# A 128-column stationary operand used as four 32-column quarters, and a copy that goes from ScalarE to VectorE, in a hybrid encoder layer

## Chip, cores and metric

The kernel runs on one core of a Trainium2 chip. The metric is the device time of one execution in microseconds (us). A core has five engines that run their own instruction queues side by side: TensorE (PE, with its weight loads shown apart as PEld), VectorE (DVE), ScalarE (ACT), GpSimd (POOL), and SyncE (SP), which here does nothing but issue DMAs. TensorE writes its results to PSUM, from where DVE and ACT take them to SBUF.

## The reference, cut to what matters

One encoder layer is applied to a prompt of 256 rows and to a sample of 2048 rows of width 1024. After a norm and one wide projection, half of the width goes through neighbourhood attention, the other half through a Fourier mix; both are normed, gated, projected out, normed again and added to the input.

```python
def fourier_mix(u, w_f, b_f):
    b, s, _ = u.shape
    ug = u.astype(jnp.float32).reshape(b, s, F_GROUPS, F_GROUP_DIM)
    spec = jnp.fft.fft2(ug, axes=(1, 3), norm='ortho')
    mixed = spec.real.reshape(b, s, F_WIDTH).astype(u.dtype)
    return mixed @ w_f + b_f

def encoder_layer(x, ...):
    h = rms_norm(x, g_pre)
    q, k, v, z_a, u_f, z_f = jnp.split(h @ w_in, ...)
    y_a = neighbourhood_attention(q, k, v, rpb)
    y_f = fourier_mix(u_f, w_fourier, b_fourier)
    mixed = jnp.concatenate([rms_norm(y_a, g_na) * jax.nn.silu(z_a),
                             rms_norm(y_f, g_f) * jax.nn.silu(z_f)], axis=-1)
    return x + rms_norm(mixed @ w_out, g_post)
```

Everything is float32. [...]

## The kernel before, in words

The program is written in the order in which TensorE works; until the third stage below the tile framework chooses the order on the other engines, except where a stretch is marked as ordered by hand. The stages in time:

1. Projections (0 to 549 us of the profile): norm, the products with `w_in`, and the first Fourier step. Results are kept in DRAM tiles (`kD`, `qD`, `vD`, `zD`, `ZD`, `uD`). Weight splits, masks and the rest of the preparation run beside it.
2. Second Fourier step (549 to 577 us, lines 1009 to 1080). `ZD` holds the first step's result, and four quarters of it, `zgs[0]` to `zgs[3]`, are loaded as four tiles of 128 x 512 each. For each quarter `gq` (called gq0 to gq3 here) and each block `c` of the 512 columns, `stage2` makes one PSUM tile `pab` of 128 x 4 x 64: four calls of `dft`, each with 128 columns of a `zg` tile as the standing operand and 64 columns of the table `d2` as the moving one. Block c = 4 is another kind: it takes 32 columns, every eighth from 256 on, and makes the same product three times, into three quarters of the partitions (c4 below). gq0 has a small extra product `pny` of one column in every block, gq2 one named `pup` of 129 columns with two accumulated matmuls. Each `pab` is then taken out of PSUM by `split_ps`: a rounded copy to `abh` (on ACT, on DVE for the first three blocks of gq0) and then the remainder to `abl` on DVE; the PSUM tile is free after the second. The tiles come from three buffers in turn (pool tag "b" has two, "c" one), so that a block waits for the third one before it to be taken out. Between the quarters stand the products `ppq` (`pq(0)` after gq2, `pq(1)` and `pq32` after gq3), which need the matrix `wf`.
3. Third Fourier step (577 to about 610 us, `y_mm` and `y_out`): for each of four row blocks e, three column tiles; PSUM buffers `py1` (three) and `py2` (two); DVE combines them into a tile `Y` (two buffers), which SP stores to DRAM. So the third `Y` (e = 2) can only be written once the store of the first has landed.
4. Attention (610 to about 860 us, the loop over `k` at line 1574), 36 groups, with the output products of the Fourier half (`po`) between them. Here the order on all engines is the order of the code. At eight places `norm_sums` adds up squares by matmuls with a matrix of ones, four standing quarters of 32 columns into `ptb[0]`, and copies the sums to SBUF (`nsb`, line 1481); `norm_turn` uses them in the next turn of the loop. `ptb[0]` is also what the next turn's transposes (`transp`, line 1505) write first, so that these wait for the copy.
5. Output products of the attention half and the last norm (860 to 969 us).

All DMAs of these stages are issued by SP in program order over eight semaphores in turn: an issue waits until the DMA eight issues before it has landed. Names in the DMA rows: `wf` is the Fourier weight (line 1005), `kl` the keys of the first head pair (line 1091, two halves), which `split_k` (line 1095) then casts on ACT in four parts to `kh`; `wo` are eight tiles of output weights (line 1234), whose buffers were those of `d2` and `zg` and so come free as TensorE goes on.

Of the kernel before, what the change touches and what calls it, by code (L numbers as in the profile page):

```python
# [168 lines left out]
def build(tc, A, O):  # L169
    nc = tc.nc  # L170
# [46 lines left out]
    def mmt(n):  # L217
        x = mmc[0] % 5 > 2
        mmc[0] += 1
        return ps.tile([128, n], F32, tag="t" if x else "a", name="mm", bufs=2 if x else 3)  # L220
# [539 lines left out]
    for b in range(16):  # L760
# [13 lines left out]
        if 2 <= b < 8:  # L774
            x, y = divmod(b, 2)
# [7 lines left out]
        p = mmt(512)[:, :TP]  # L783
# [3 lines left out]
        o = st.tile([128, 256], F32, tag="f", name="f", bufs=3)  # L787
        if kind % 2:
            i, d = p, o
        else:  # L790
            i = p.rearrange("p (b r c) -> p b r c", b=2, c=32)
            d = o.rearrange("p (r b c) -> p b r c", b=2, c=32)
# [46 lines left out]
    for i in range(16):  # L839
# [15 lines left out]
        o = [st.tile([128, 1024], F32, tag="f", name="f", bufs=3) for x in range(2)]  # L855
# [32 lines left out]
        for j in range(7):  # L888
# [29 lines left out]
            if sg == 0:  # L918
                x, y = divmod(7 * (pr - 1) + j, 14)
# [17 lines left out]
            for f, d in ((u_load, 0), (u_split, 4), (u_stage1, 6)):  # L937
                x = 7 * pr + j - 7 - d
# [11 lines left out]
            p = mmt(512)  # L950
# [39 lines left out]
    ptb = [ps.tile([128, 512], F32, tag="t", name="ptb", bufs=2) for i in range(2)]  # L990
# [24 lines left out]
    def split_ps(dh, dl, src, vec=False):  # L1015
        nc.vector.tensor_copy(dh, src) if vec else nc.scalar.copy(dh, src)
        nc.vector.tensor_tensor(out=dl, in0=src, in1=dh.bitcast(F32), op=ALU.subtract)

    def dft(p, c, pairs):
        sts = [(p[32 * r:32 * r + 32], slice(256, 512, 8)) for r in range(3)] if c == 4 else \  # L1020
            [(p, slice(c * 128, c * 128 + 128))]
        for out, cols in sts:
            for x, (z, d) in enumerate(pairs):
                nc.tensor.matmul(out, z[:, cols], d, start=x == 0, stop=x == len(pairs) - 1)  # L1024


    def split_ab(gq, c, view, p):
# [7 lines left out]
    def stage2(gq, zg, c):  # L1035
        m = int(c in (2, 3))
        np_ = 96 if c == 4 else 128
        x = (gq * 5 + c) % 3 == 2
        p = ps.tile([np_, 4, 64], F32, tag="c" if x else "b", name="pab", bufs=1 if x else 2)
        for g in range(4):  # L1040
            dft(p[:, g, :], c, [(zg[g], d2[gq // 2][:, (gq % 2) * 4 + g, m * 64:m * 64 + 64])])
        split_ab(gq, c, lambda a: a[:, :1024].rearrange("p (k q g l) -> p q g k l", k=16, q=4, g=4)[:, gq],
                 p.rearrange("p g (k l) -> p g k l", l=4))
        if gq == 0:
            p = ps.tile([np_, 1], F32, tag="a", name="pny")
            dft(p, c, [(zg[0], dnyq[:, m:m + 1])])
            split_ab(gq, c, lambda a: a[:, 1024:1025], p)
        if gq == 2:
            p = ps.tile([np_, 129], F32, tag="a", name="pup")
            dft(p, c, [(up[:, t], f256[:, t, 129 * m:129 * m + 129]) for t in range(2)])  # L1050
            split_ab(gq, c, lambda a: a[:, 1025:1154], p)
# [192 lines left out]
    for t, (g, x) in enumerate(zip(G, (0, 640))):  # L1244
        g["w"] = []
        for c0, w in g["t"]:
            n = 2 * g["nr"] * w
# [228 lines left out]
    def norm_sums(sq, ts):  # L1476
        n = 32 * len(ts)
        for x, t in enumerate(ts):
            nc.tensor.matmul(ptb[0][32 * x:32 * x + 32, :128], ones32, sq[:, t * 128:t * 128 + 128], start=True, stop=True)
        o = sm.tile([128, 128], F32, name="nsb", bufs=1)[:n]  # L1480
        nc.scalar.copy(o, ptb[0][:n, :128])  # L1481
        nsb.append(o)

    def norm_turn(dst, ts):
# [89 lines left out]
    for k in range(2, len(G) + 1):  # L1574
# [21 lines left out]
        x = k // 2 + 1  # L1596
# [52 lines left out]
        if k + 1 in NT:  # L1649
            norm_sums(sqs if k < 31 else ysq, NT[k + 1])  # L1650
# [8 lines left out]
        if 32 <= k < 36:  # L1659
            x, d = k - 32, atiles[k - 32]  # L1660
# [122 lines left out]
```

## Time and profile before

| | us |
|---|---|
| median of three runs (lowest 971.94, highest 977.72) | 972.99 |
| the profiled execution | 970.48 |
| its span from the first to the last instruction | 968.7 |
| TensorE busy in the span | 958.9 |
| VectorE busy | 709.5 |
| ScalarE busy | 497.5 |
| GpSimd busy | 430.2 |

The mean clock granted to TensorE is 0.998 of full speed. The profiled execution is 1.8 us longer than its span, and 2.5 us below the median. Rows of a timeline give the start, the duration, the engine, the source line, the operation, what is written and read, the sizes, and how many instructions are merged into the row; a bracket at the end tells how long the engine had been idle and what ended it. "128\*32" before the size of a matmul means that 128 rows and 32 columns of the array are used.

### The profile page before, as it was taken

The page shows a single profiled execution, that of the slowest core. Times are in us where ns is not written, and L with a number is a line of the kernel's source. Part 1 is how long each engine was busy: PE and PEld are TensorE (multiplying, and loading weights), DVE is VectorE, ACT ScalarE, POOL GpSimd, SP SyncE. Part 2 cuts the span into 40 slices and gives each one's busy share as a digit, 9 for nine tenths or more (in the row PEclk, how much of TensorE's full clock was granted, in tenths as well). Part 3 has the DMA queues.
Part 4 walks back from the last instruction along what each step waited for, and adds up shares of the span by engine and source line. Part 5 has one row for each costly group of instructions (what it writes and reads, how often), then busy time and mean ns, then how long its engine had stood idle before and what let it go on. Part 6 is the DMA issues. An engine that isn't in the chain of part 4 may idle for free.

```text
span 968.7 us, 17031 instructions
## 1 busy us (share of the span) xinstructions
PE 958.9 (99%) x5769; PEld 801.0 (83%) x5769; DVE 709.5 (73%) x1306; ACT 497.5 (51%) x1078; POOL 430.2 (44%) x400
## 2 busy tenths in 40 slices
PE   9999999999999999999999999999999999999997
PEld 7889988888888888888888879887788888878886
DVE  6768987777986867787777446776665656649997
ACT  6836675433325533333344255677666776744443
POOL 3100003464752202756654033577677686624544
PEclk9999999999999999999999999999999999999999
DMA  9899696556849996599989898698887998979993
GB/s 327 312 373 357 234 366 240 194 189 252 318 163 377 352 410 239 211 371 320 322 303 339 301 328 300 210 281 273 258 240 234 286 327 270 296 244 331 330 346 129
DMA packets 146450, 279.89 MB, mean 289 GB/s; under 512 B 13162, under 2 KB 84284, under 8 KB 142972
## 3 DMA queue, kind: packets, MB, share of 16 engines
q1 hardware_dynamic: 145932, 278.41, 82.4%
q8 instruction: 46, 0.75, 0.3%
q10 hardware_dynamic: 432, 0.39, 0.1%
q14 instruction: 40, 0.33, 0.1%
HBM read 184.37 MB, written 101.72 MB: 295 GB/s over the span
## 4 chain that ended last, share of the span: by engine, by line
PE 96%; DVE 1%; ACT 1%; issue 1%; POOL 1%; DMA 0%; DVEq 0%; SPq 0%; POOLq 0%; ACTq 0%
PE po L1432 19%; PE mm L165 18%; PE mm L164 18%; PE mm L166 18%; PE pv L1521 5%; PE ptb L1505 5%; PE s L1181 4%; PE pab L1024 2%; PE py L164 1%; PE py L166 1%; PE py L165 1%; DMA gpre<-gpre 0%; PE ppq L1062 0%; PE pz L166 0%; PE pz L164 0%
## 5 line engine op out<-in xcount | busy, mean ns | idle before, releaser
L164 PE MATMUL mm<-xh,wa 128*128 128x512 f32 x448 | 174.4, 389 | 0.0
L165 PE MATMUL mm<-xl,wa 128*128 128x512 f32 x448 | 174.3, 389 | 0.0
L166 PE MATMUL mm<-xh,wa 128*128 128x512 f32 x448 | 174.3, 389 | 0.0
L536 POOL TENSOR_TENSOR ws<-wr 128x512 f32<-128x512 f32 x16 | 22.2, 1386 | 226.6 <-DMA wr<-wz 222.8
L1215 POOL TENSOR_SCALAR w<-w,m 128x480 f32<-128x480 f32 (+6 forms) x136 | 86.0, 644 | 46.3 <-DVE m L1212 35.9
L164 PEld LDWEIGHTS mm<-xh,wa 128*128 128x128 f32 x448 | 84.1, 188 | 17.6
L166 PEld LDWEIGHTS mm<-xh,wa 128*128 128x128 f32 x448 | 84.1, 188 | 17.5
L165 PEld LDWEIGHTS mm<-xl,wa 128*128 128x128 f32 x448 | 84.1, 188 | 17.4
L1432 PE MATMUL po<-wo,yh 128*128 128x512 f32 x272 | 90.4, 413 | 0.0
L551 DVE TENSOR_TENSOR wa<-wr,wa 128x512 fp32r<-128x512 f32 x60 | 68.5, 1149 | 27.1 <-ACT wa L550 26.8
L1208 ACT ACTIVATE w<-w,m 128x480 f32<-128x480 f32 (+6 forms) x136 | 79.3, 586 | 17.1 <-DVE m L1203 17.1
L1432 PE MATMUL po<-w,yh 128*128 128x512 f32 x280 | 86.7, 391 | 0.0
L1203 DVE CUSTOM_DVE_ANT_1 w<-s,tb 128x360 f32<-128x360 f32 (+5 forms) x124 | 62.4, 541 | 10.3 <-PE s L1181 9.8
L589 POOL TENSOR_TENSOR mt<-mt,rmask 128x880 f32<-128x880 f32 (+2 forms) x24 | 51.0, 2139 | 34.1 <-DVE mt L585 27.6
L165 PE MATMUL mm<-vl,xh 128*128 128x512 f32 x168 | 65.5, 390 | 0.2 <-DVE vl L482 0.2
L164 PE MATMUL mm<-vh,xh 128*128 128x512 f32 x168 | 65.4, 389 | 0.0
L166 PE MATMUL mm<-vh,xl 128*128 128x512 f32 x168 | 65.4, 389 | 0.0
L877 DVE TENSOR_TENSOR f<-u,mm 128x512 f32<-128x512 f32 x64 | 43.5, 680 | 28.0 <-PE mm L166 23.1
L1432 PEld LDWEIGHTS po<-w,yh 128*128 128x128 f32 x280 | 52.3, 188 | 10.9 <-issue 0.2
L1505 PE MATMUL ptb<-ident,w 128*120 128x128 f32 (+5 forms) x428 | 59.5, 276 | 1.0 <-ACT nsb L1481 0.9
L550 ACT CAST wa<-wr 128x512 fp32r<-128x512 f32 x60 | 36.4, 617 | 44.1 <-PE mm L166 23.2
L1521 PEld LDWEIGHTS pv<-pt,v 120*64 120x64 f32 (+6 forms) x896 | 48.2, 136 | 12.8 <-issue 9.6
(263 smaller groups left out, 2394.3 us busy)
## 6 DMA issues: line engine op xcount, KB each, us to landing
wr<-wz SPq DMA_DIRECT2D x48, 512.0 KB
vl<-sD SPq DMA_DIRECT2D x20, 512.0 KB
xm<-xm SPq DMA_DIRECT2D x9, 1024.0 KB
oD<-ofs SPq DMA_DIRECT2D x18, 512.0 KB
of<-oD SPq DMA_DIRECT2D x18, 512.0 KB
yr<-yD SPq DMA_DIRECT2D x34, 256.0 KB
zD<-f SPq DMA_DIRECT2D x16, 512.0 KB
woD<-wo SPq DMA_DIRECT2D x16, 512.0 KB
```

Source lines behind the costliest of these rows:

```text
L164: nc.tensor.matmul(out, lh, rh, start=first, stop=False)
L165: nc.tensor.matmul(out, lh, rl, start=False, stop=False)
L166: nc.tensor.matmul(out, ll, rh, start=False, stop=last)
L551: nc.vector.tensor_tensor(out=o[:, 1], in0=src, in1=o[:, 0].bitcast(F32), op=ALU.subtract)
L589: nc.gpsimd.tensor_tensor(out=o, in0=i, in1=rmask[:, m0:m0 + n].unsqueeze(2).to_broadcast([128, n, 80]), op=ALU.add)
L877: nc.vector.tensor_tensor(out=dst(f, b), in0=src(uu[u]), in1=src(p), op=op)
L1203: nc.vector.tensor_tensor_reduce(out=rows(g["w"][b][:, h, :n], w), in0=rows(g["s"][2 * b + h][:, :n], w), in1=tv, scale=1.0, scalar=3.0e38 ...
L1208: nc.scalar.activation(w, w, AF.Exp, bias=m[:, h:h + 1], scale=-1.0, accum_out=m[:, 2 + h:3 + h])
L1215: nc.gpsimd.tensor_scalar(w, w, m[:, 4 + h:5 + h], 1.0, ALU.mult, ALU.mult)
L1432: nc.tensor.matmul(p, (d["l"] if x == 2 else d["h"])[:, c], w(n, int(x == 1), c), start=j == 0, stop=j == 11)
L1505: nc.tensor.transpose(ptb[h][:nk, j * 128:j * 128 + 128], g["w"][b][:, h, c0:c0 + nk], ident)
L1521: nc.tensor.matmul(p[hs, b], g["v"][:nk, v, hs], g["pt"][b][:nk, h, j * 128:j * 128 + 128], start=j == 0, stop=j == len(ch) - 1)
```

## The change

In `dft` the standing operand of 128 columns is no longer one matmul that writes all 128 partitions of the PSUM tile. It is used as four slices of 32 neighbouring columns, and each slice's matmul writes its own 32 partitions. The loop over the accumulated pairs is now outside, the loop over the slices inside; for c4, which had three slices already, only this order is different, and only in `pup`, the one product with two pairs. What is computed, and into which elements of PSUM, stays the same. `pab`, `pny` and `pup` all go through `dft`. Apart from it, the copy of the norm's sums in `norm_sums` goes from ScalarE to VectorE.

```diff
     def dft(p, c, pairs):
-        sts = [(p[32 * r:32 * r + 32], slice(256, 512, 8)) for r in range(3)] if c == 4 else \
-            [(p, slice(c * 128, c * 128 + 128))]
-        for out, cols in sts:
-            for x, (z, d) in enumerate(pairs):
-                nc.tensor.matmul(out, z[:, cols], d, start=x == 0, stop=x == len(pairs) - 1)
+        sts = [slice(256, 512, 8)] * 3 if c == 4 else [slice(c * 128 + 32 * r, c * 128 + 32 * r + 32) for r in range(4)]
+        for x, (z, d) in enumerate(pairs):
+            for r, cols in enumerate(sts):
+                nc.tensor.matmul(p[32 * r:32 * r + 32], z[:, cols], d, start=x == 0, stop=x == len(pairs) - 1)
...
-        nc.scalar.copy(o, ptb[0][:n, :128])
+        nc.vector.tensor_copy(o, ptb[0][:n, :128])
```

Where this moves instructions is shown by three pieces of the instruction order, a minus for before and a plus for now. The first is TensorE around the end of the second Fourier step, from the last `pup` of gq2 over `pq(0)`, gq3 and `pq(1)` to `pq32`.

```order
 L1024 MATMUL pup<-f_4859,up 32x129 x6
 L1062 MATMUL ppq<-wf,cs_4869 64x512 x4
-L1024 MATMUL pab<-d_4719,zg 128x64 x16
-L1024 MATMUL pab<-d_4719,zg 32x64 x12
+L1024 MATMUL pab<-d_4719,zg 32x64 x76
 L1062 MATMUL ppq<-wf,cs_4869 64x512 x4
 L1069 MATMUL ppq<-wf,c_4871 96x512 x4
```

The sixteen wide matmuls of gq3 have become sixty-four narrow ones, and nothing has changed its place among its neighbours. The second piece is ScalarE at the same place, where the framework chooses the order: the casts of gq3's blocks (`abh`) and of the keys (`kh`).

```order
 L1016 CAST pqh<-ppq 128x512
-L1016 CAST abh_4875<-pab 128x4x16x4 x2
+L1016 CAST abh_4875<-pab 128x4x16x4
+L1095 CAST kh<-kl 128x576
+L1016 CAST abh_4875<-pab 128x4x16x4
+L1095 CAST kh<-kl 128x576
 L1016 CAST abh_4877<-pab 128x4x16x4
-L1095 CAST kh<-kl 128x576 x2
+L1095 CAST kh<-kl 128x576
 L1016 CAST abh_4877<-pab 128x4x16x4
-L1095 CAST kh<-kl 128x576
 L1031 CAST a_4879<-pab 96x4x16x4
```

The second cast of keys has moved from behind gq3's third block to behind its first, the third to behind the second, and the fourth to behind the third. On VectorE the order of a few rows of gq0 is different, and none has moved past another block. The third piece is VectorE at the last of the eight places of `norm_sums`, between the product with the gate (`y`) and the copy of the second half of the transposes (`pt`).

```order
 L1212 RECIPROCAL m<-m 128x2
 L1535 TENSOR_TENSOR y<-pv,za 128x2x8x16
+L1481 COPY nsb<-ptb 128x128
 L1509 COPY pt<-ptb 128x384
 L1380 TENSOR_SCALAR ds<-pn 128x4
```

The copy now stands directly behind the product with the gate; on ScalarE it stood behind the square of `pv`, and is gone there.

## The prediction, made before the changed kernel ran

> **What bounds the kernel now.** I read the page first, then who waits for whom, then the timeline of each engine through the second Fourier step. The page says that TensorE is the bound: it is busy for the whole span and makes up almost the whole chain that ended last.
>
> ```profile
> PE 958.9 (99%) x5769; PEld 801.0 (83%) x5769; DVE 709.5 (73%) x1306; ACT 497.5 (51%) x1078; POOL 430.2 (44%) x400
> ...
> PE 96%; DVE 1%; ACT 1%; issue 1%; POOL 1%; DMA 0%; DVEq 0%; SPq 0%; POOLq 0%; ACTq 0%
> ```
>
> So TensorE time that is taken out should come off the end, unless something that TensorE has outrun until now becomes late. The next fence is TensorE's timeline through the stage that `dft` fills.
>
> ```profile
> 549.14 1.00 PE L1024 MATMUL pab<-d,zg 128*128 128x64 f32 x8
> 549.97 0.33 PE L1024 MATMUL pny<-dnyq,zg 128*128 128x1 f32 x2
> 550.17 1.08 PE L1024 MATMUL pab<-d,zg 128*128 128x64 f32 x8
> ...
> 553.59 0.72 PE L1024 MATMUL pab<-d,zg 128*32 128x64 f32 x24
> 554.14 0.24 PE L1024 MATMUL pny<-dnyq,zg 128*32 128x1 f32 x6
> 554.31 5.48 PE L1024 MATMUL pab<-d,zg 128*128 128x64 f32 x64
> 559.62 0.66 PE L1024 MATMUL pup<-f,up 128*128 128x129 f32 x4
> 560.12 1.00 PE L1024 MATMUL pab<-d,zg 128*128 128x64 f32 x8
> 560.97 0.66 PE L1024 MATMUL pup<-f,up 128*128 128x129 f32 x4
> ...
> 564.79 0.68 PE L1024 MATMUL pup<-f,up 128*32 128x129 f32 x12
> 565.40 1.94 PE L1062 MATMUL ppq<-wf,cs 128*64 128x512 f32 x8
> 567.26 4.44 PE L1024 MATMUL pab<-d,zg 128*128 128x64 f32 x56
> 571.64 1.94 PE L1062 MATMUL ppq<-wf,cs 128*64 128x512 f32 x8
> ```
>
> What something costs here is the distance to the next row's start, since records overlap. A wide block of eight records costs 0.83 (549.14 to 549.97) to 0.85 us (560.12 to 560.97). The row of x64 holds five wide blocks and a c4 and lasts to 559.62, 5.31 us. The row at 553.59 is what the change makes of the rest: c4 already uses 32 columns at a time, and its 24 records cost 0.55 us.
>
> **Step 1: a narrow block.** A wide block becomes 32 records. If quarters of the array run beside each other, those are eight groups of four, as c4 is eight groups of three. Two rows show that they do; the second is a shorter window on the first.
>
> ```profile
> 857.20 0.43 PE L1479 MATMUL ptb<-ysq,ones 128*32 128x128 f32 x8
> ...
> 857.20 0.32 PE L1479 MATMUL ptb<-ysq,ones 128*32 128x128 f32 x4
> ```
>
> Four quarters of 128 moving columns begin so close together that all four are over in 0.32 us, and two such groups of four are over in 0.43: four go as one. So I take c4's 0.55 us for a narrow block. The other end is that the records and not the groups set the pace: 0.55 / 24 = 23 ns each, 0.73 us a block. I take 0.55, since the rows with four quarters are nearest. `pny` costs 0.20 us wide (549.97 to 550.17) and 0.17 in c4; `pup` 0.50 wide (559.62 to 560.12) and 0.61 in c4, of which part is the change of shape to `ppq`. I put both at nothing (between a gain of 0.03 and a loss of 0.11 for each of four).
>
> Free of all else the blocks would gain: gq1 with the first block of gq2 5.31 - 0.55 - 5 x 0.55 = 2.0 us; three blocks of gq2 3 x (0.85 - 0.55) = 0.9; gq3 (567.26 to 571.64, 4.38 with a c4) 4.38 - 5 x 0.55 = 1.6; gq0 4 x (0.83 - 0.55) = 1.1.
>
> **Step 2: what becomes late in gq0 to gq2.** In gq0 DVE takes the blocks out.
>
> ```profile
> 551.06 0.40 DVE L1016 CAST abh<-pab 128x256 fp32r<-128x256 f32 x1
> ...
> 552.75 0.41 DVE L1017 TENSOR_TENSOR abl<-pab,abh 128x256 fp32r<-128x256 f32 x1
> ```
>
> DVE works without a break from 551.06, and c4 needs the buffer that is free after the subtraction at 552.75, 553.16. It began at 553.59, so gq0 gains 0.4 and not 1.1. TensorE would then reach `pq(0)` at 565.40 - 0.4 - 2.0 - 0.9 = 562.1. But `pq(0)` needs `wf`. SP's waits and its timeline show when that landed.
>
> ```profile
> SPq L1135 <- DMA kl<-kD: 2.0, 1, 2.0
> SPq L1159 <- DMA wf<-wf: 1.9, 1, 1.9
> ...
> 562.79 0.34 SPq L1159 DMA_DIRECT2D za<-zD  x1
> 565.18 0.38 SPq L1135 DMA_DIRECT2D ql<-qD  x1
> 566.63 1.03 SPq L1152 DMA_DIRECT2D v<-vD  x2
> ```
>
> SP's issue at 562.79 (L1159) had waited for `wf`, those at 565.18 and 566.63 for the two halves of the keys. Nothing in this row of DMAs waits for a `dft`, so they land when they did. `pq(0)` starts at 562.8: a gain of 2.6, whichever of step 1's prices holds down to arrivals at 562.8.
>
> **Step 3: gq3 behind the casts of keys.** gq3 starts at 562.8 + 1.86 (565.40 to 567.26) = 564.7. ACT now has a cast of keys ahead of each of its blocks, and the first cannot start before 565.18.
>
> ```profile
> 567.00 0.68 ACT L1095 CAST kh<-kl 128x576 fp32r<-128x576 f32 x1
> 567.58 0.59 ACT L1016 CAST pqh<-ppq 128x512 fp32r<-128x512 f32 x1
> 568.41 0.37 ACT L1016 CAST abh<-pab 128x256 fp32r<-128x256 f32 x1 [0.24 <-PE pab L1024]
> ```
>
> At 0.58 a cast of keys (567.00 to 567.58), 0.5 for `pqh` and 0.3 for a block, the second block's cast starts at 565.18 + 0.58 + 0.5 + 0.3 + 0.58 = 567.1, its remainder on DVE is done at 567.1 + 0.4 + 0.4 = 567.9, and only then does c4 have a buffer; it ends at 568.5. `pq(1)` began at 571.64: the gain is 3.1. Ends: 2.6, if gq3 gains nothing, and 2.6 + 1.6 = 4.2, if ACT does not hold it.
>
> **Step 4: the store of the first Y.** In the third Fourier step TensorE is ahead of DVE, which waits for a DMA once. After the two timeline rows stand waits of SP, and then two windows, which end with the share that the DMA engines were busy and GB/s.
>
> ```profile
> 594.21 1.34 DVE L1276 TENSOR_TENSOR Y<-t,py 128x252 f32<-128x252 f32 x7 [2.00 <-DMA yD<-Y]
> ...
> 596.44 0.34 PE L164 MATMUL py<-abh,pqh 128*128 128x384 f32 x1
> ...
> SPq L1234 <- PE py L1263: 1.2, 1, 1.2
> ...
> SPq L1234 <- PE ppq L1062: 1.0, 1, 1.0
> ...
> 575.00:580.00 5.00, 5.00 (x23) 3.70 (x22) 0.68 (x1) 1.07 (x2) 3.26 (x4) 1.00 0.94 273
> 580.00:585.00 5.00, 5.00 (x30) 5.00 (x30) 3.33 (x12) 1.70 (x4) 0.00 (x0) 1.00 1.04 391
> ```
>
> The product at 596.44 writes the buffer that this DVE row frees at 595.55. Moved up by 3.1 it is due at 593.3, and waits 2.2 if the store lands when it did. The store stands in the DMA queues behind the loads of `wo`, and those waited 2.2 us for TensorE. From 575 to 580 the core moved 273 GB/s, later 391: (391 - 273) x 5 us is 590 KB, 1.5 us of transfers that can move up. The buffer is then free at 594.05, and TensorE gives back 0.7. What stays is 2.4; ends 0.9 (the store does not move) and 3.1, or 4.2 with step 3's. After it I find no DMA that TensorE waits for, and the shift should reach the end.
>
> **Step 5: the copy of the sums.** These rows are the last of the eight places.
>
> ```profile
> 857.32 0.42 DVE L1535 TENSOR_TENSOR y<-pv,za 128x256 f32<-128x256 f32 x1 [2.22 <-PE pv L1521]
> ...
> 858.12 0.26 ACT L1481 COPY nsb<-ptb 128x128 f32<-128x128 f32 x1
> ...
> 858.52 0.85 PE L1505 MATMUL ptb<-ident,w 128*128 128x128 f32 x6 [0.89 <-ACT nsb L1481]
> ...
> PEld ptb L1505 <- ACT nsb L1481: 0.6, 2, 0.4
> ...
> 560.62 0.29 DVE L1017 TENSOR_TENSOR abl<-pup,abh 128x129 fp32r<-128x129 f32 x1
> ```
>
> DVE is free at 857.74; its nearest operation in size takes 0.29. So the copy is done at 858.03 and not 858.38, a gain of 0.35. Two other waits, 0.6 together, shrink as well; I take 0.5 for all. The other end of the gain is 0.9 + 0.6 = 1.5. Against it: at seven places the copy stands ahead of the next scores' row operations on DVE and delays those by 0.29. I cost that at nothing, because TensorE does the transposes and half an output product meanwhile; without that cover it is 7 x 0.29 = 2.0.
>
> **Sum.** 2.4 + 0.5 = 2.9 us off the profiled execution's 970.48 gives 967.6. The median lies 2.5 above that execution, 972.99, so I predict 970.1 us.
>
> **Rivals.** *The records set the pace.* At 23 ns a record `pq(0)` comes at 565.40 - 0.4 - 5 x 0.22 - 3 x 0.12 = 563.5, later than `wf`; gq3 then ends at 565.4 + 4 x 0.73 + 0.55 = 568.9, a gain of 2.8 where step 3 had 3.1. With step 4 nearly nothing changes: 970.2 to 971. The Trainium skill, "TensorE: Matmul & The Clock Gate", section "Wait — 56ns, not 53.3ns?", has such a floor: starts never closer than about 25 ns. An estimate by that page is 32 x 25 = 0.80 us a block. The trace agrees with its average over c4, not with single starts: four in 0.32 us.
>
> *The gain is hidden.* The store does not move (0.9 stays), or another transfer is late, and the DVE copies take it: 972 to 974. For it speaks a DMA share of 0.94 to 1.04 around 580, against it that TensorE's loads of `wo` were held by TensorE.
>
> *Slower: quarters run one after the other.* If a narrow record costs what a wide one does (0.83 / 8 = 0.104), a block costs 3.3 us, 16 of them +38, with `pup` (16 records for 4, +1.5 each) and `pny` (+0.6 each) +47: 1020 us. It decides from 0.9 / 32 = 28 ns a record on; c4 has 23 and the rows of four speak against it.
>
> **How the numbers follow.** About 1% of this kernel, 10 us, is what a measurement can tell from no change. Chances: the forecast 0.60, records 0.15, hidden 0.20, one after the other 0.03, and 0.02 for a gain over 1%, for which no row has the time. Range: all gains at their ends, 4.2 + 1.5, give 967.3; 0.9 less 2.0 give 974.1. I take 967 to 974. Faster 0.02, same 0.95, slower 0.03.
>
> **What would show it.** Right: starts of neighbouring `pab` blocks 0.5 to 0.6 apart in gq1; TensorE idle ahead of `pq(0)`, ended by `wf` near 562.8; `pq(1)` near 568.5; the third `Y` near 592.7; the transposes of 858.52 begin 0.35 sooner after the matmuls with ones. Wrong: blocks of 0.73 or over; no wait at `pq(0)`; a shift of the whole that is lost again before 620.

## The result, and the profile after

| | before | after |
|---|---|---|
| median of the runs side by side, us | 972.66 (971.25 to 977.72, 6 runs) | 982.07 (978.73 to 985.08, 6 runs) |
| the profiled execution, us | 970.48 | 979.09 |
| its span, us | 968.7 | 977.3 |
| mean clock granted to TensorE | 0.998 | 0.992 |

The changed kernel takes 1.009 times as long, with a 95% interval of 1.006 to 1.0119: slower by some 9 us, where a gain of 2.9 was forecast. Here are three lines of the page of the kernel after: busy time, the DMA queue that I read as the one for TensorE's instructions (packets, MB, share; the table of packets below bears this out), and the chain that ended last; behind them the same queue on the page of the kernel before.

```profile
PE 956.8 (98%) x6225; PEld 797.0 (82%) x6225; DVE 709.0 (73%) x1314; ACT 496.1 (51%) x1070; POOL 429.7 (44%) x400
...
q8 instruction: 50, 0.82, 0.3%
...
PE 93%; DMA 2%; issue 2%; DVE 1%; SPq 1%; ACT 1%; POOL 1%; DVEq 0%; ACTq 0%; POOLq 0%
```

```profile
q8 instruction: 46, 0.75, 0.3%
```

TensorE is busy 2.1 us less than before, and yet the span is 8.6 us longer: TensorE is idle 10.7 us more. 76 wide matmuls have become 304, and each leaves two records in the trace, so TensorE has 456 more records, each with a weight load of its own, and the instruction queue brought four packets more. One packet is 0.82 MB / 50, 16 KB.

The next fence is TensorE's timeline of the kernel after through the second Fourier step, the place of the prediction's second fence.

```profile
550.31 0.65 PE L1024 MATMUL pab<-d,zg 128*32 128x64 f32 x32
550.84 0.63 PE L1024 MATMUL pab<-d,zg 128*32 128x64 f32 x32
551.35 0.63 PE L1024 MATMUL pab<-d,zg 128*32 128x64 f32 x32
...
553.15 0.65 PE L1024 MATMUL pab<-d,zg 128*32 128x64 f32 x32 [1.14 <-DVE abl L1017]
...
554.82 1.42 PE L1024 MATMUL pab<-d,zg 128*32 128x64 f32 x84
559.98 3.04 PE L1024 MATMUL pab<-d,zg 128*32 128x64 f32 x99 [3.74 <-issue]
...
566.15 0.75 PE L1024 MATMUL pab<-d,zg 128*32 128x64 f32 x19 [1.89 <-issue]
...
572.62 0.43 PE L1024 MATMUL pup<-f,up 128*32 128x129 f32 x3 [2.58 <-issue]
...
574.90 2.27 PE L1062 MATMUL ppq<-wf,cs 128*64 128x512 f32 x8
577.10 1.32 PE L1024 MATMUL pab<-d,zg 128*32 128x64 f32 x79
579.39 1.38 PE L1024 MATMUL pab<-d,zg 128*32 128x64 f32 x73 [0.97 <-issue]
580.70 1.94 PE L1062 MATMUL ppq<-wf,cs 128*64 128x512 f32 x8
```

The narrow block is what was hoped for: 0.51 us from 550.84 to 551.35 with its `pny`, where a wide one took 1.03 (549.14 to 550.17). But after 84 records from 554.82 on, TensorE stands still for 3.74 us, and then for 1.89, 2.58 and 0.97: 9.2 us in four spells, all put down to "issue", that is, to nothing that the profile shows: no tile, no buffer, no transfer of data. Between the end of one spell and the beginning of the next stand 127, 128 and 128 records. `pq(0)` starts 24.59 us after the step's first block (574.90 - 550.31), before 16.26 (565.40 - 549.14). `pq(1)` comes at 30.39 (580.70 - 550.31) instead of 22.50, 7.9 later, and that is still 7.4 at the last place of `norm_sums` (below). The loss arises in these 25 us; the other 1.2 us by which the span is longer lie ahead of the step, which begins at 550.31 instead of 549.14 though the change lies behind that place.

The table of windows of the kernel after shows what comes with the idle time; the third number from the end is the granted clock, then come the DMA engines' share and GB/s.

```profile
557.00:560.00 3.00, 0.02 (x4) 0.02 (x4) 0.00 (x0) 0.00 (x0) 0.00 (x0) 0.76 1.01 364
560.00:564.00 4.00, 4.00 (x127) 4.00 (x127) 1.69 (x4) 1.49 (x4) 0.00 (x0) 0.50 1.04 401
564.00:568.00 4.00, 2.11 (x63) 1.88 (x61) 0.72 (x3) 0.73 (x3) 0.00 (x0) 0.50 1.03 412
```

From 557 to 560 no engine does anything to speak of; the DMA engines are full. Behind it the clock is 0.50 for 8 us, so that the records that did arrive ran at half speed: 127 of them took 4 us. From spell to spell this costs little. Spells end 6.2 and 6.5 us apart here (559.98, 566.15, 572.62), and just as far apart in the kernel tiny_busy below, where 128 records last only 1.9 us: records that last longer make the spell shorter.

### The profile page after: what moved, and what is told of

The parts are those of the page before. It is cut to its first block, busy times and chain, and to the rows that moved or that the text cites. A ratio compares the mean times of both kernels' runs of the same rounds, so it can differ in the third digit from the quotient of the medians.

```text
span 977.3 us, 17944 instructions
## 1 busy us (share of the span) xinstructions
PE 956.8 (98%) x6225; PEld 797.0 (82%) x6225; DVE 709.0 (73%) x1314; ACT 496.1 (51%) x1070; POOL 429.7 (44%) x400
## 4 chain that ended last, share of the span: by engine, by line
PE 93%; DMA 2%; issue 2%; DVE 1%; SPq 1%; ACT 1%; POOL 1%; DVEq 0%; ACTq 0%; POOLq 0%
PE po L1432 20%; PE mm L165 17%; PE mm L164 17%; PE mm L166 17%; PE pv L1521 5%; PE ptb L1505 5%; PE s L1181 4%; PE pab L1024 1%; PE py L164 1%; PE py L166 1%; DMA wr<-wz 1%; PE py L165 1%; DMA gpre<-gpre 0%; PE pup L1024 0%; PE ppq L1062 0%
## 5 line engine op out<-in xcount | busy, mean ns | idle before, releaser
L551 DVE TENSOR_TENSOR wa<-wr,wa 128x512 fp32r<-128x512 f32 x60 | 70.8, 1186 | 27.4 <-ACT wa L550 27.3
```

The lines of the kernel that those rows point to most:

```text
L551: nc.vector.tensor_tensor(out=o[:, 1], in0=src, in1=o[:, 0].bitcast(F32), op=ALU.subtract)
```

## Experiments

Times stand beside runs of the kernel before on the same chip: 971.6 us for the first four kernels, 972.67 for copy_only, gq13 and halves, 972.42 for gq12, halves_wo and before_wo, 972.47 for the last two. tiny_busy, tiny_quiet, after_quiet and gq12 were executed once each. The profiled executions reach the second Fourier step up to 3 us apart, so times inside the step are counted from its first `pab` block: 549.14 in the kernel before.

My theory after the result: TensorE's instructions come by DMA in pieces of 16 KB. A piece is 128 records with their weight loads, a wide record lasts 0.104 us, so that 128 last 13 us, but narrow ones at 0.51 us for 40 use a piece up in less than 2 us, and under the loads of this stage a piece takes longer than that.

**dft_only.** The quarters alone; the sums are copied on ScalarE as before.

```diff
-        nc.vector.tensor_copy(o, ptb[0][:n, :128])
+        nc.scalar.copy(o, ptb[0][:n, :128])
```

> The change without its second part: the quarters stay, the copy of the sums is back on ScalarE. Theory A (instruction pages): TensorE stalls because its instructions come in pieces of 16 KB, 256 instructions or 128 records with their weight loads, and narrow records use up a piece in 2 to 3 us while the next takes about 6; then the whole loss sits in the Fourier stage, the four idle spells of 3.74, 1.89, 2.58 and 0.97 us appear again at the same records, and the time is 982 us, within 1 of the changed kernel. Theory B (the copy on VectorE delays the attention stage): most of the 9 us is gone, 973 to 975 us.

982.0 us, a ratio of 1.0114 (1.0097 to 1.0131), with idle spells of 4.01, 1.89 and 2.88 us ahead of `pq(0)`. The fourth did not come back: the clock was down at `pq(0)`, which took 3.61 us (574.96 to 578.57) instead of 2.20; the packet landed at 577.91, before TensorE needed it. The quarters are the loss; the copy has no part in it that these runs could tell.

**tiny_busy and tiny_quiet.** Into the kernel before come 240 small products (480 records) that nobody reads, in quarters, right behind `pq(0)`. They wait for no data. In tiny_quiet the keys and all loads behind them are held until the step's last result is out, so that the DMA engines have nothing else to do.

```diff
+            pbu = ps.tile([128, 1], F32, tag="a", name="pbu")
+            for y in range(60):
+                for r in range(4):
+                    nc.tensor.matmul(pbu[32 * r:32 * r + 32], zgs[2][0][:, 32 * r:32 * r + 32], dnyq[:, :1], start=True, stop=True)
```

The loads are held by a small write into the keys' tile that needs the step's last result, ahead of the keys' load in tiny_quiet, with SyncE's DMAs there in the order of the code.

```diff
+        nc.vector.tensor_copy(KK[0][1][:96, x * (T // 2):x * (T // 2) + 1], a32[:, 1023:1024].bitcast(F32))
```

> The kernel before (wide blocks), with 240 extra matmuls of one moving column and 32 standing columns (480 records, 960 instructions) behind the first ppq products; nobody reads their result, and nothing waits for a table or a buffer there. Theory A: 184 of the records run at once, the other 296 at the pace of the pieces, 6.2 us for 128, with idle spells at every 128th record: the burst takes 15 to 19 us, and the total rises by 14 to 18 us to about 988. Theory C (records cost only their own time): no spells, at 12 to 28 ns a record 6 to 13 us.

> The same burst with the later loads held back as in after_quiet, so that the DMA engines are nearly idle in it. Theory A with a fetch that stands behind data: spells remain at every 128th record, but a piece takes 2.5 to 4 us and the burst 8 to 11 us. Theory A with a fetch of fixed duration: the same 15 to 19 us as in tiny_busy. Theory C: the same 6 to 13 us without spells. The total is no measure, because what follows gets its loads late.

997.39 and 1002.18 us; what matters is the burst, not the sum, since in tiny_quiet the held loads come late for all that follows. tiny_busy was expected at 988: its burst took 19.0 us (569.60 to 588.62), the upper end of what was expected, and behind it gq3 ran at the lowered clock, 8.0 us (588.62 to 596.65) instead of 4.4. The burst of tiny_quiet took 12.1 us, one more than expected. TensorE's timeline of tiny_busy, and behind it the window of its burst:

```profile
569.60 1.71 PE L1081 MATMUL pbu<-dnyq,zg 128*32 128x1 f32 x184
575.32 1.89 PE L1081 MATMUL pbu<-dnyq,zg 128*32 128x1 f32 x128 [4.01 <-issue]
581.79 1.89 PE L1081 MATMUL pbu<-dnyq,zg 128*32 128x1 f32 x128 [4.58 <-issue]
587.98 0.71 PE L1081 MATMUL pbu<-dnyq,zg 128*32 128x1 f32 x40 [4.31 <-issue]
588.62 8.10 PE L1024 MATMUL pab<-d,zg 128*128 128x64 f32 x56
```

```profile
570.00:588.00 18.00, 5.10 (x415) 4.84 (x405) 0.86 (x2) 2.22 (x5) 6.99 (x5) 0.64 0.88 275
```

The same of tiny_quiet:

```profile
568.93 1.71 PE L1081 MATMUL pbu<-dnyq,zg 128*32 128x1 f32 x184
573.25 1.89 PE L1081 MATMUL pbu<-dnyq,zg 128*32 128x1 f32 x128 [2.61 <-issue]
576.98 1.89 PE L1081 MATMUL pbu<-dnyq,zg 128*32 128x1 f32 x128 [1.84 <-issue]
580.43 0.71 PE L1081 MATMUL pbu<-dnyq,zg 128*32 128x1 f32 x40 [1.57 <-issue]
```

```profile
570.00:581.00 11.00, 4.98 (x372) 4.72 (x362) 0.36 (x1) 0.00 (x0) 0.00 (x0) 0.59 0.02 4
```

Products that need nothing but their instructions stop after 184 records, as expected, and then after exactly 128, again and again. With 275 GB/s of transfers a period is 6.2 to 6.5 us (575.32 to 581.79 to 587.98), with 4 GB/s, which are the instruction packets themselves, 3.5 to 3.7.

The stops are places in the program. In each of these kernels 2591 records of TensorE come before the step's first `pab`. Counted from there, the bursts of tiny_busy and tiny_quiet both stop behind record 402, 530 and 658, after behind 274, 401, 529 and 657, gq12 (below) behind 274 and 402, and halves once, behind 273; where the count is one less, a record may be missing from the trace. These kernels differ in what TensorE computes there, in shape and in data, and they stop at the same counts, 128 apart. The packets of the instruction queue, read from the trace one by one (us), show what ends a stop; "resumes" is the start of TensorE's next record.

```
            packet starts   lasts   TensorE resumes
after          557.75        0.99       559.98
               563.75        0.91       566.15
               569.85        1.28       572.62
               576.93        1.03       579.39
tiny_busy      572.75        1.17       575.32
               579.23        1.11       581.79
               585.47        1.12       587.98
tiny_quiet     570.93        0.92       573.25
               574.37        1.41       576.98
               578.11        1.11       580.43
```

Every spell ends 1.2 to 1.5 us after a packet has landed. The next packet starts 3.7 to 4.3 us after TensorE has resumed when other transfers run, and 1.1 us after it when none do. So a packet is asked for when the piece ahead of it is begun, then stands in line with the other transfers, lands, and is ready: 3.8 + 1.1 + 1.4 = 6.3 us, or 1.1 + 1.3 + 1.2 = 3.6 in the quiet. That the request goes with the begin of a piece is inferred from these distances. It can come somewhat ahead of the piece's first record: in the kernel before a packet starts at 549.20, and that record at 551.09.

The Trainium skill describes this in "Runtime: NRT & Kernel Launch", section "Instruction fetch mechanics": 16 KiB blocks of 256 instructions, the next one fetched over a DMA queue while the current one is executed. On this the traces agree. It also says that the cost of crossing a block is mostly hidden; here it was 3.74, 1.89, 2.58 and 0.97 us.

**after_quiet.** The kernel after, with the same loads held.

> The changed kernel, but all loads behind that of the Fourier weight (keys, bias tables, values, output weights) wait until the last block of the second Fourier step is out of PSUM, so that the DMA engines have little to do from about 563 us on. The loads come late for what follows, so the total is no measure; what counts is the second Fourier step. Theory A with a fetch that stands behind data in the DMA engines: the first idle spell, before 560 us, stays at 3 to 4 us; the later ones (1.89, 2.58, 0.97) shrink to under 1 us each, and a piece of 128 records takes under 4.5 us instead of about 6.2. Theory A with a fetch of fixed duration: the later spells stay as they are. Theory C (TensorE waits for PSUM buffers or for tables): the spells stay and do not fall on every 128th record.

TensorE's timeline, the rows behind the spells:

```profile
560.79 3.04 PE L1024 MATMUL pab<-d,zg 128*32 128x64 f32 x99 [4.56 <-issue]
566.41 0.48 PE L1024 MATMUL pab<-d,zg 128*32 128x64 f32 x19 [1.34 <-issue]
570.41 0.31 PE L1024 MATMUL pup<-f,up 128*32 128x129 f32 x3 [1.36 <-issue]
```

990.79 us in all, from the held loads. The first spell is no shorter, since the loads that this step itself needs (`zg`, `f`, `up`, `wf`) still run there; once they are through, a period is 4.0 us (566.41 to 570.41) where after has 6.5. The later spells were expected under 1 us and are 1.34 and 1.36. The spells ahead of `pq(0)` come to 7.3 us instead of 8.2. Holding loads back is no cure.

**copy_only.** The kernel before with the copy of the sums on VectorE.

> The second part of the change alone: the copy of the norm's sums on VectorE, wide blocks as before. The prediction's step 5: 0.5 us faster, between 1.5 faster and 2.0 slower; the wait at the last of the eight places falls from 0.89 to about 0.5 us. The rival that VectorE is delayed: 1 to 2 us slower, with new waits of TensorE for VectorE in the attention stage.

972.05 us, a ratio of 0.9995 (0.9984 to 1.0006): no difference that 12 runs can tell. What it does at one place shows at the last of the eight places, here in the kernel after, to be held against the prediction's rows at 858.12 and 858.52:

```profile
866.70 0.29 DVE L1481 COPY nsb<-ptb 128x128 f32<-128x128 f32 x1
867.13 0.84 PE L1505 MATMUL ptb<-ident,w 128*128 128x128 f32 x6 [0.57 <-DVE nsb L1481]
```

TensorE waits 0.57 us where it waited 0.89; copy_only has the same 0.57 at 860.34.

**gq13.** Quarters in gq1 and gq3 only, with the copy on VectorE. This keeps 152 of the narrow records together in gq1 and 152 in gq3, with wide work between.

```diff
-            dft(p[:, g, :], c, [...])
+            dft(p[:, g, :], c, [...], 32 if gq in (1, 3) else 128)
```

> Quarters in gq1 and gq3 alone, wide blocks in gq0 and gq2, copy on VectorE. Eight narrow blocks instead of sixteen, with slow wide work ahead of each group and behind it. Theory A: 152 records in a row fit in the piece that is at hand and the one ahead, so there is no spell or one under 1 us, each narrow block costs 0.55 instead of about 0.95 us, and the total is 2 to 3.5 us below the kernel before, about 970. Theory C (a narrow record is slow in itself): half of the loss, about 977.

972.79 us, a ratio of 1.0 (0.9989 to 1.0012). TensorE's timeline, from several windows:

```profile
551.15 1.00 PE L1027 MATMUL pab<-d,zg 128*128 128x64 f32 x8
...
566.43 1.94 PE L1065 MATMUL ppq<-wf,cs 128*64 128x512 f32 x8 [0.76 <-DVE a L1036]
...
571.48 1.94 PE L1065 MATMUL ppq<-wf,cs 128*64 128x512 f32 x8
...
598.81 0.42 PE L164 MATMUL py<-abh,pqh 128*128 128x384 f32 x1 [2.36 <-DVE Y L1279]
```

No spell for instructions is left. `pq(1)` comes 20.33 us after the first block, 2.2 sooner than before. Then TensorE stands 2.36 us at the third `Y`, and nothing is left of the gain: about 970 was expected.

**gq12.** The same with gq1 and gq2, so that the narrow records stand in one stretch.

```diff
-            ..., 32 if gq in (1, 3) else 128)
+            ..., 32 if gq in (1, 2) else 128)
```

> Quarters of 32 columns in the two neighbouring groups gq1 and gq2 only, gq0 and gq3 wide as before, the sums copied on VectorE. Theory A (TensorE's instructions come in pieces of 16 KB, 128 narrow records each, a piece is asked for when the one ahead of it is begun, and takes about 6.3 us under the loads of this stage): gq1 and gq2 have about 350 narrow records behind the start of a piece, so two idle spells of about 4 us each that end every 128 records; pq(0) starts near 571 to 573 instead of 567.4 (the start of gq0 as in the kernel gq13), and the time is 975 to 979. Rival (narrow records cost nothing as long as there are only as many as in gq13, where 315 of them cost no idle spell, wherever they stand): no spell, pq(0) near 566.4 as in gq13, 972 to 973.

978.44 us, where 975 to 979 was expected. TensorE's timeline:

```profile
564.31 0.58 PE L1027 MATMUL pab<-d,zg 128*32 128x64 f32 x26 [3.29 <-issue]
...
570.51 0.53 PE L1027 MATMUL pup<-f,up 128*32 128x129 f32 x10 [2.01 <-issue]
...
572.32 3.26 PE L1065 MATMUL ppq<-wf,cs 128*64 128x512 f32 x8
```

Two spells, 128 records apart, and `pq(0)` at 572.32, where 571 to 573 was expected; the spells are 5.3 us and not 8. gq12 has 434 narrow records in the step and gq13 370, so it is not their number that costs, but how many stand together: 184 pass in tiny_busy and 274 in after before the first spell, and every 128 behind them wait. How many pass depends on where they begin: the burst of tiny_busy begins 56 records ahead of the end of a piece (record 274), 56 + 128 = 184; after begins 18 ahead of one, 18 + 2 x 128 = 274.

**halves.** Two slices of 64 columns everywhere, with the copy on VectorE; 152 more records than before instead of 456.

```diff
-            dft(p[:, g, :], c, [...])
+            dft(p[:, g, :], c, [...], 64)
```

> Two halves of 64 columns instead of four quarters in all wide blocks: 442 records in the stage instead of 290 before and 746 with quarters. Theory A: a block of 16 records takes about 0.56 us, so that 128 records are used up in 4.5 us, and pieces need about 6: short spells of 1 to 2 us between, which eat about what the blocks gain, total within 2 us of the kernel before. If the number of records did not matter: 3 us faster, as the prediction had it.

971.42 us, a ratio of 0.9986 (0.9975 to 0.9998). TensorE's timeline, from several windows:

```profile
551.76 0.69 PE L1027 MATMUL pab<-d,zg 128*64 128x64 f32 x16
552.36 0.67 PE L1027 MATMUL pab<-d,zg 128*64 128x64 f32 x16
...
562.80 0.57 PE L1027 MATMUL pab<-d,zg 128*64 128x64 f32 x13 [0.40 <-issue]
...
566.56 1.94 PE L1065 MATMUL ppq<-wf,cs 128*64 128x512 f32 x8 [1.64 <-DVE a L1036]
...
571.71 1.51 PE L1065 MATMUL ppq<-wf,cs 128*64 128x512 f32 x6
...
597.94 0.42 PE L164 MATMUL py<-abh,pqh 128*128 128x384 f32 x1 [1.26 <-DVE Y L1279]
```

A block in halves takes 0.60 us with its `pny` (551.76 to 552.36), nearly as good as quarters, and the spells, expected at 1 to 2 us, shrink to one of 0.40. The rest is the prediction's steps 2 to 4. SyncE's and VectorE's timelines of halves:

```profile
558.37 0.43 SPq L1005 DMA_DIRECT2D wf<-wf  x1
...
566.49 0.34 SPq L1162 DMA_DIRECT2D za<-zD  x1
```

```profile
596.45 2.33 DVE L1279 TENSOR_TENSOR Y<-t,py 128x252 f32<-128x252 f32 x10 [4.17 <-DMA yD<-Y]
```

SyncE's issue at 566.49 had waited for `wf`, and `pq(0)` starts with it, though the row names VectorE, whose work on `a` was over by 565.6. `pq(1)` comes 19.95 us after the first block, 2.55 sooner than before. The store of the first `Y` lands 44.69 us after the first block (596.45 - 551.76), before 45.07, so it moved up by only 0.4; TensorE waits 1.26 us for it, and 1.1 us of the gain remain at 597.94.

**halves_wo and before_wo.** To see whether the loads of `wo` hold that store: four of the eight go behind it, in halves and in the kernel before.

```diff
-    for n in range(2):
+    def load_wo(n):
         for c in range(4):
...
+    load_wo(0)
...
             nc.sync.dma_start(yD[1, e, :, TP:], Y[:, TP:])
+            if e == 0:
+                load_wo(1)
```

> The kernel with halves, and four of the eight loads of wo (2 MB) issued behind the store of the first Y instead of ahead of it. In halves TensorE was 2.3 us ahead at pq(1) and the third Y then waited 4.17 us for the store of the first, after which 0.9 us were left. Theory (step 4's other end: the store lands when the wo loads ahead of it are through): 2 MB at about 390 GB/s are 5.4 us, the store lands 5 us sooner, VectorE does not wait for it, TensorE has no idle time at the product that took 1.26 us there, 2.2 to 2.4 us stay and the time is 969.5 to 970.5, against 971.4 of halves. Rival (the loads of wo that come later are late for the output products, or other transfers hold the chain): 971.4 or more, with an idle spell of TensorE for wo after 608.

> The kernel before with only that change in the order of the loads of wo. Theory: TensorE does not wait at the third Y in the kernel before, so there is nothing to gain: 972.0 to 973.2. Rival (the order of the loads is a gain by itself): 971.5 or less, and then the gain of halves_wo is not the halves'.

973.48 us, a ratio of 1.0005 (0.999 to 1.002), and 975.22 us, 1.0021 (1.0005 to 1.0036): neither as expected. The wait at the third `Y` is gone in halves_wo, as the theory had it, but the framework also put the large store of the third `Y` ahead of the load of `y0`. In before_wo the order is the same; GpSimd waits 5.88 us for `y0` there, and TensorE 0.54 and 1.00 us at 613 to 615. GpSimd, ScalarE and TensorE of halves_wo wait in turn for `y0`:

```profile
606.21 1.02 POOL L1330 TENSOR_TENSOR y<-y 128x384 f32<-128x384 f32 x1 [6.51 <-DMA y<-yD]
...
607.25 0.62 ACT L1358 CAST y0h<-y 128x512 fp32r<-128x512 f32 x1 [3.76 <-POOL y L1330]
...
607.92 3.30 PE L1440 MATMUL po<-wo,y0h 128*128 128x512 f32 x12 [0.73 <-ACT y0h L1358]
```

**halves_wo2 and before_wo2.** Only two loads of `wo` behind the store, and SyncE's other DMAs in the order of halves.

```diff
-    load_wo(0)
+    load_wo(range(6))
...
+    spo.enter_context(tc.manual_schedule(engines={mybir.EngineType.SP}))
...
             if e == 0:
-                load_wo(1)
+                load_wo((6, 7))
```

> The kernel with halves, two of the eight loads of wo (1 MB, 2.6 us at 390 GB/s) behind the store of the first Y, and SyncE's other DMAs in the order of halves (in halves_wo the large store of the third Y had also come ahead of the load of y0). Theory: the store lands 2.6 us sooner than in halves, near 593.8, before TensorE needs the buffer; the DMA queues do not run empty; no idle time of TensorE near 597 (1.26 us in halves) nor for y0h at 607 (0.73 us in halves_wo); the shift from pq(1) on is kept through the third Fourier step, and the time is 969.5 to 970.5. Rival (the gain is lost to the next transfer in the queue, the second Y or y0): 971 to 972 with a new idle spell of TensorE between 600 and 620.

> The kernel before with the same change in the order of SyncE's DMAs and nothing else. Theory: TensorE does not wait for the third Y in the kernel before, so 972 to 973. Rival (the order is worth something by itself): 971.4 or less, and halves_wo2 owes its gain to it; or 974 and more as in before_wo, if it was the loads of wo, and not the load of y0 behind the third Y, that cost time there.

970.99 us, a ratio of 0.9979 (0.997 to 0.9988), and 972.75 us, 1.0003 (0.9993 to 1.0013). The order alone is worth nothing; with halves it gives the best kernel of the study, though by less than I expected and by no more over halves than two separate comparisons can tell. VectorE's, GpSimd's and TensorE's timelines of halves_wo2 say where the rest went:

```profile
593.54 1.34 DVE L1282 TENSOR_TENSOR Y<-t,py 128x252 f32<-128x252 f32 x7 [2.07 <-DMA yD<-Y]
```

```profile
603.47 1.01 POOL L1332 TENSOR_TENSOR y<-y 128x384 f32<-128x384 f32 x1 [4.96 <-DMA y<-yD]
```

```profile
609.79 0.39 PE L1516 MATMUL ptb<-ident,kh 128*80 128x128 f32 x2 [0.24 <-POOL ql L1167]
611.18 0.39 PE L1516 MATMUL ptb<-ident,kh 128*80 128x128 f32 x2 [1.00 <-DVE pt L1520]
```

The store landed where it was expected, 2.1 us sooner after the first block than in halves (593.54 - 550.91 = 42.63 against 44.69), and TensorE has no wait at 597. But now `y0` is 1.9 us later than in halves (603.47 - 550.91 = 52.56 against 602.40 - 551.76 = 50.64) and no sooner than before (601.66 - 549.14 = 52.52), and 1.24 us go at 610 to 611 where 1.26 went at 597. The same two waits of TensorE are in halves_wo and before_wo, where `y0` comes later still, and not in halves. The third Fourier step here ends with its transfers, whichever of them comes last.

## Why the prediction was wrong

It forecast a gain of 2.9 us and 967 to 974 us; the median is 982.07, a loss, and no rival had the cause. The ratio of 1.009 does lie within the 1% on which it put 0.95, but that is luck: the working gives no loss of 9 us. Nor is 1% too little to be told from no change: the interval of 1.006 to 1.0119 lies clear of 1.

- **What bounds the kernel, and step 1.** This is the step that failed: "TensorE time that is taken out should come off the end, unless something that TensorE has outrun until now becomes late." What became late was TensorE's own instructions. I had counted the added records by their time on the array (0.55 us a block), and put the bringing of 456 records with 456 loads at nothing, without a reason; it cost four idle spells, 9.2 us. The row that would have told was on the page of the kernel before: 46 packets and 0.75 MB for 5769 records, one packet for about 125. The four quarters were to become 722 records (608 of `pab`, 76 of `pup`, 38 of `pny` in the trace after), between five and six packets, in less than 20 us.
- **Step 1's price** was right, or a little high: 0.51 us with `pny` in gq0, and 84 records of gq1 in 1.2 us up to the first spell, 0.45 a block, against 0.55. The first rival, that records set the pace, falls for the block by itself: 40 records in 0.51 us are 13 ns each. The Trainium skill's floor of about 25 ns between starts ("TensorE: Matmul & The Clock Gate", section "Wait — 56ns, not 53.3ns?") would give 0.80 us for a block's 32, as an estimate; the trace does not show it across four quarters. The mechanism that did decide gives 6.3 / 128 = 49 ns a record, which is past the 28 ns that I had named as the point from which the change loses. That rival, quarters one after the other, had a chance of 0.03, another cause and 47 us.
- **Step 2** had gq0 held by VectorE ahead of c4, with 0.4 us of gain: it was held, for 1.14 us ahead of its fourth block and 0.16 ahead of c4, and gained 0.7 (554.82 - 550.31 = 4.51 against 554.31 - 549.14 = 5.17). The wait for `wf` does not exist in the kernel after, since TensorE comes 10 us too late. In halves and gq13, where instructions keep up, it is there. `wf` was issued as long after the first block as before (6.61 us, 555.75 before) but landed 14.73 us after it instead of 13.65, so that "they land when they did" was 1.1 us too kind: the gain at `pq(0)` was 1.5 in halves (566.56 - 551.76 = 14.80 against 16.26) and not 2.6.
- **Step 3** gave 3.1 at `pq(1)`; halves has 2.55 and gq13 2.2.
- **Step 4** had the store of the first `Y` move up by 1.5 us and 2.4 stay, with 0.9 if it did not move. It moved by 0.4 in halves, and 1.1 stayed. In gq13 it came 1.1 us later than before (597.32 - 551.15 = 46.17; the row there names ScalarE, but the trace has the store's landing 0.12 us ahead of VectorE's start, as in before and halves), and nothing stayed. So versions with one short spell or none come to the lower end of step 4, or to the rival that the gain is hidden (972 to 974): 971.4 and 972.8.
- **Step 5** was right at its place: 0.32 us less wait instead of 0.35, with a copy of 0.29. In the time of the whole kernel it cannot be seen.

## What to carry to other kernels

Cutting one matmul into several narrow ones multiplies instructions, and these have to be brought: count the records that a stretch uses per microsecond against the time of a piece (here 128 records with their loads in 6.3 us beside full DMA queues, 3.6 in idle ones), and look in the profile for idle time put down to "issue" at even distances in records. The first 184 to 274 short records passed free here, depending on where in a piece they began, so keep short ones in such groups with long ones between, or take the coarser cut: halves had 0.60 us a block where quarters had 0.51, and a third of the extra records. And where a stage ends with its transfers, a faster engine waits at the next one in the queue: 1.26 us at the third `Y` became 1.24 us at `y0`.

## What the runs showed of the hardware

- A block with its `pny` takes 0.51 us in four quarters (40 records), 0.60 in two halves (20) and 1.03 whole (10): four narrow records together take 51 ns, one wide record 103, so quarters overlap one another.
- Instructions of TensorE come 128 records with their weight loads at a time: after, gq12 and both bursts stop every 127 or 128 records, at the same counts from the step's first record, and each stop in the table of packets ends 1.2 to 1.5 us after a packet has landed.
- A packet of 16 KB takes about 1.1 us, but after a stop 3.7 to 4.3 us pass before the next one starts when other transfers fill the queues (after and tiny_busy; 3.2 and 3.7 in gq12), and 1.1 us when they do not (tiny_quiet).
- Behind the spell of 3.74 us in the kernel after the granted clock is 0.50 for 8 us, and with the spells of tiny_busy it is 0.64 on the mean over the burst; records then run at half speed, those of gq3 behind that burst too. It does not follow every wait: gq13 has a clock of 1.00 from 595 to 606, around its wait of 2.36 us.
